# Where the halves of the weights are kept, how the block inverses are grouped, and which queue loads the weights

## The chip, the cores and the metric

The kernel runs on one core of a Trainium2 chip. A core has five engines that run side by side: TensorE (PE, matrix products into PSUM; PEld is its loading of the stationary operand), VectorE (DVE), ScalarE (ACT), GpSimd (POOL) and SyncE (SP, which issues transfers and computes nothing). Each executes its own list of instructions in order, and semaphores order the lists against one another. Transfers between DRAM and SBUF run on 16 DMA engines, whichever engine issued them.

The metric is the device time of one execution in microseconds. Of several executions the median is given.

## The reference, cut to what matters

One layer of a decoder on 2048 tokens of width 1024, all float32. A combined projection feeds three mixers; their outputs, side by side, go through w_out, a layer norm, a gated feed-forward with a depthwise convolution, and a second layer norm.

```python
proj = h @ w_in
y_a = _gated_deltanet(a_qkv, a_z, a_b, a_dec, conv_w, a_log, dt_bias, norm_w)
y_b = _dilated_window_group(b_qkv)
y_c = _diff_attention_group(c_qkv, lam_vecs, diff_norm_w, lam_init)
y = jnp.concatenate([y_a, y_b, y_c], axis=-1) @ w_out
x = _layer_norm(DEEPNORM_ALPHA * x + y, ln1_g, ln1_b)
u = _causal_depthwise_conv(x @ w_up, conv_w); gate, val = jnp.split(u, 2, axis=-1)
f = (jax.nn.silu(gate) * val) @ w_down
x = _layer_norm(DEEPNORM_ALPHA * x + f, ln2_g, ln2_b)
```

The gated delta rule (4 heads of 128) is computed by chunks. In each chunk a unit lower triangular system with the matrix I + m has to be solved, where m holds products of keys, scaled and decayed, below the diagonal; then a state of 128 x 128 for each head passes from chunk to chunk:

```python
a_mat = jnp.eye(C) + m
u = triangular_solve(a_mat, v * beta);  w = triangular_solve(a_mat, k_beta * exp(g))
def step(S, inp):
    v_new = u_i - w_i @ S
    o = q_i @ S + qk_i @ v_new
    S = S * exp(gl_i) + kt_i.T @ v_new
```

## The kernel before, in words

The 2048 tokens are four blocks of 512. Each product with a weight of 1024 x 128 (`Dense.product`, lines 182 to 184) is 8 x 3 matmuls of 512 columns: weight and activation are both split into a rounded high half and the rest, the low half, and three of the four cross products are added up.

`Dense.weights` brings a weight's halves into SBUF. On the raw path (lines 129 to 133) it loads 512 KB (`wraw`), ScalarE casts the high half (`whi`, line 132) and POOL subtracts it to get the low half (`wlo`, line 133). Where the weight has a key and `dn.keep` is set, both halves are also stored to DRAM (line 137), and a later use of the same weight loads the two halves, 512 KB each, with no arithmetic (lines 124 to 128, the kept path). `keep` is set from job A1 on (line 1292). All loads and stores are issued by SyncE. The buffers of weights are seven tiles of 512 KB (`NW`), shared by raw tiles and halves.

The work is a list of jobs in three stages (`FIRST`, `SECOND`, `THIRD`, lines 1341 to 1343):

- A0 to A3: projection of one block for the two attention mixers, eight products and the values (lines 628 to 630, which take each of the four `w_val` weights twice); 12 different weights in all.
- G0 to G3: projection of one block for the delta rule, 16 products, each followed by a convolution on VectorE (lines 336 to 344), and for queries and keys a square that POOL splits (lines 350 and 352).
- i0 to i3 (`invert`): for the four chunks of 128 tokens of a block, the products of keys (line 426), the mask with decay, and the inverses of the 32 x 32 blocks on the diagonal. These are solved on VectorE for all heads and chunks of the block at once, one block in one partition, so on 64 partitions, by 31 steps of a multiplication (line 441) and a subtraction (line 443). The blocks go through DRAM to be regrouped (`blk_d`, `x_d`).
- b0 to b7 (`merge`): for two chunks, the 32 x 32 inverses are put together into 128 x 128 inverses on TensorE.
- p0 to p7 (`prepare`), r0 to r7 (`recur`): for two chunks, transposes and query-key products, and then the recursion, whose state passes from r0 to r7 in order.
- d and w: the two attentions of a block; c0: the first pool is closed and the feed-forward's constants begin; o0: w_out and the first norm for block 0; t0: its transpose; f0 to f3: feed-forward of a block, in which the next block's w_out is done as well.

The list gives priorities and not times. A scheduler, which simulates the program as it is built, places each engine's instructions in an order of its own, so that products of a later job stand between those of an earlier one; that order is fixed when the kernel runs. `flush` emits the small pieces of work that were put off.

## Time and profile before

| | |
|---|---|
| median of 3 runs | 3292.46 us (3285.46 to 3297.71) |
| the profiled execution | 3287.69 us, span of its instructions 3285.8 us |
| PE busy | 3039.0 us, 92% |
| DVE busy | 1940.7 us, 59% |
| ACT busy | 1251.7 us, 38% |
| POOL busy | 493.0 us, 15% |
| mean granted TensorE clock | 0.955 |
| moved by DMA | 701.06 MB, 213 GB/s |

A row of a view by stretches gives the length, the busy microseconds of each engine with the number of instructions, the granted TensorE clock as a share of full speed, the mean busy share of the 16 DMA engines, and GB/s. A row of a view of groups gives line, engine, operation, output<-input tiles, shapes and count; then busy us and mean ns of one; then the engine's idle time just before them and what ended it. A row of a view of waits says which instruction waited for which: us in all, times, longest. SPq is SyncE's list.

### The profile page before, as it was taken

Reading aid. Unit: us, or ns where it says so; the run is one execution under the profiler, and the core shown is the slowest. Engines: PE = TensorE matmul, PEld = TensorE weight load, DVE = VectorE, ACT = ScalarE, POOL = GpSimd, SP = SyncE. Lnnn points to the kernel's source line nnn. Section 1 sums busy time; section 2 is a strip of 40 time slices with the busy share of each in tenths; the row PEclk is TensorE's granted clock in tenths of the full one; section 3 lists DMA queues with packets and bytes.
Section 4 is the critical chain, followed back from the end, with each engine's and each line's share of the span. In section 5 each row is a group of like instructions: output and inputs, shape, how many; then the busy total and the mean of one; then the engine's idle time right before and its main releaser. Section 6 shows DMA issues by size and latency. Waiting matters only on the chain.

```text
span 3285.8 us, 41437 instructions
## 1 busy us (share of the span) xinstructions
PE 3039.0 (92%) x14476; PEld 2335.1 (71%) x14476; DVE 1940.7 (59%) x3738; ACT 1251.7 (38%) x2735; POOL 493.0 (15%) x342
## 2 busy tenths in 40 slices
PE   7888687999978888998999999999999999999998
PEld 5666576787767667666776667777788666788887
DVE  2564177858544536755887645565897444474446
ACT  2644143353324315644655422232655333221113
POOL 3452252111102003333312000000000000000001
PEclk8899898999988989999999999999999999999999
DMA  6437776766778878766785655555775444665553
GB/s 190 144 132 263 262 257 218 222 208 200 242 253 276 289 246 265 245 225 209 269 281 198 232 187 177 180 184 173 238 261 201 148 162 144 209 236 192 192 188 139
DMA packets 365281, 701.06 MB, mean 213 GB/s; under 512 B 63024, under 2 KB 189488, under 8 KB 364304
## 3 DMA queue, kind: packets, MB, share of 16 engines
q1 hardware_dynamic: 365072, 698.41, 64.0%
q8 instruction: 115, 1.88, 0.2%
q14 instruction: 94, 0.77, 0.1%
HBM read 525.99 MB, written 172.16 MB: 212 GB/s over the span
## 4 chain that ended last, share of the span: by engine, by line
PE 57%; DMA 7%; DVE 4%; ACT 2%; issue 2%; SPq 1%; POOL 0%; ACTq 0%; POOLq 0%; DVEq 0%
PE d L184 9%; PE d L183 9%; PE d L182 9%; PE rp L1131 6%; PE rp L1132 6%; PE rp L1134 5%; PE bank L791 4%; PE bank L806 2%; DMA wraw<-in_w_up 2%; DMA wlo<-wlo_d 2%; PE bank L970 1%; PE bank L740 1%; PE bank L977 1%; PE bank L931 1%; DMA wraw<-in_w_down 1%
## 5 line engine op out<-in xcount | busy, mean ns | idle before, releaser
L182 PE MATMUL d<-xhi,whi 128*128 128x512 f32 x2144 | 872.4, 408 | 54.7 <-DVE i_halo L336 18.1
L184 PE MATMUL d<-xhi,wlo 128*128 128x512 f32 x2144 | 866.4, 404 | 22.4 <-DMA wlo<-wlo_d 18.2
L183 PE MATMUL d<-xlo,whi 128*128 128x512 f32 x2144 | 864.9, 403 | 1.8 <-DVE xlo L145 1.7
L182 PEld LDWEIGHTS d<-xhi,whi 128*128 128x128 f32 x2144 | 416.9, 195 | 164.0 <-issue 20.3
L133 POOL TENSOR_TENSOR wlo<-wraw,whi 128x1024 fp32r<-128x1024 f32 x137 | 337.1, 2461 | 1207.7 <-ACT whi L132 1067.8
L184 PEld LDWEIGHTS d<-xhi,wlo 128*128 128x128 f32 x2144 | 415.9, 194 | 131.8 <-DMA wlo<-wlo_d 20.4
L183 PEld LDWEIGHTS d<-xlo,whi 128*128 128x128 f32 x2144 | 416.6, 194 | 105.8 <-issue 18.2
L1131 PE MATMUL rp<-whi,hhi 128*128 128x512 f32 x704 | 278.6, 400 | 6.0 <-DVE r L1141 2.3
L1132 PE MATMUL rp<-wlo,hhi 128*128 128x512 f32 x704 | 279.3, 397 | 0.0
L1134 PE MATMUL rp<-whi,hlo 128*128 128x512 f32 x672 | 263.0, 397 | 0.0
L132 ACT CAST whi<-wraw 128x1024 fp32r<-128x1024 f32 x137 | 143.6, 1048 | 281.0 <-DMA wraw<-in_w_gdn 65.2
L749 ACT ACTIVATE bank<-bank,nm 128x512 f32<-128x512 f32 (+3 forms) x320 | 190.3, 595 | 110.8 <-DVE nm L745 72.7
L745 DVE TENSOR_REDUCE nm<-bank 128x1 f32<-128x512 f32 (+3 forms) x288 | 165.4, 596 | 72.6 <-PE bank L740 70.4
L1063 ACT COPY ub<-d 128x512 f32<-128x512 f32 x172 | 100.7, 586 | 265.4 <-PE d L184 264.7
L812 DVE SCALAR_TENSOR_TENSOR pd<-pe,f_nlam,pd 128x512 f32<-128x512 f32 (+3 forms) x160 | 123.5, 786 | 124.4 <-ACT pe L808 81.5
L816 POOL TENSOR_SCALAR_AFFINE_SELECT pd<-pd 128x128 f32<-128x128 f32 x64 | 29.8, 472 | 1018.0 <-DVE pd L812 990.6
L1131 PEld LDWEIGHTS rp<-whi,hhi 128*128 128x128 f32 x704 | 133.2, 189 | 43.4 <-issue 6.3
L1132 PEld LDWEIGHTS rp<-wlo,hhi 128*128 128x128 f32 x704 | 133.3, 189 | 35.0 <-issue 8.5
L1141 DVE TENSOR_TENSOR r<-r,rp 128x512 f32<-128x512 f32 x152 | 102.3, 684 | 84.1 <-PE rp L1134 77.4
L1134 PEld LDWEIGHTS rp<-whi,hlo 128*128 128x128 f32 x672 | 127.0, 189 | 33.0 <-issue 6.5
L1064 DVE COPY c_halo<-d 128x2 f32<-128x2 f32 x172 | 26.8, 156 | 205.2 <-ACT ub L1063 205.0
L1068 DVE SCALAR_TENSOR_TENSOR yg<-ub,c_taps,yg 128x512 f32<-128x512 f32 x176 | 144.8, 823 | 3.6
(280 smaller groups left out, 4723.2 us busy)
## 6 DMA issues: line engine op xcount, KB each, us to landing
whi<-whi_d SPq DMA_DIRECT2D x291, 512.0 KB
wlo<-wlo_d SPq DMA_DIRECT2D x291, 512.0 KB
whi_d<-whi SPq DMA_DIRECT2D x101, 512.0 KB
wlo_d<-wlo SPq DMA_DIRECT2D x101, 512.0 KB
ks<-fk_d SPq DMA_DIRECT2D x160, 196.0 KB
wraw<-in_w_up SPq DMA_DIRECT2D x43, 512.0 KB
wraw<-in_w_gdn SPq DMA_DIRECT2D x32, 512.0 KB
wraw<-in_w_down SPq DMA_DIRECT2D x25, 512.0 KB
```

The lines of the kernel that those rows point to most:

```text
L132: nc.scalar.copy(hi, raw)
L133: nc.gpsimd.tensor_tensor(out=lo, in0=raw, in1=hi, op=ALU.subtract)
L182: nc.tensor.matmul(out=ps, lhsT=whi[:, k], rhs=xhi[k], start=(k == 0), stop=False)
L183: nc.tensor.matmul(out=ps, lhsT=whi[:, k], rhs=xlo[k], start=False, stop=False)
L184: nc.tensor.matmul(out=ps, lhsT=wlo[:, k], rhs=xhi[k], start=False, stop=(k == KD - 1))
L745: nc.vector.tensor_reduce(out=o, in_=s[:, 0:nf], axis=mybir.AxisListType.X, op=ALU.min)
L749: nc.scalar.activation(out=s[:, 0:n], in_=s[:, 0:n], func=AF.Exp, scale=-1.0, bias=o, accum_out=den[:, b, m, qt : qt + 1])
L791: nc.tensor.matmul(out=po[64 * hh : 64 * hh + 64, q0:], lhsT=v[:, 64 * hh : 64 * hh + 64], rhs=pd[hh][:, q0:], start=start, stop=stop)
L1068: nc.vector.scalar_tensor_tensor(out=yc, in0=ub[:, j : j + TB], scalar=self.taps[:, mt, j : j + 1], in1=yc, op0=ALU.mult, op1=ALU.add)
L1131: nc.tensor.matmul(out=ps, lhsT=hi[:, sl], rhs=whi, start=first, stop=False)
L1132: nc.tensor.matmul(out=ps, lhsT=hi[:, sl], rhs=wlo, start=False, stop=last and lo is None)
L1134: nc.tensor.matmul(out=ps, lhsT=lo[:, sl], rhs=whi, start=False, stop=last)
```

## The change

- Loads of weights, raw tiles and kept halves, are issued by POOL (`nc.gpsimd.dma_start`) and no longer by SyncE. Stores of halves stay with SyncE.
- `keep` is set at job c0 and no longer at A1. In the new order c0 stands behind G3, ahead of i1. So A1, G1, G2 and G3 take the raw path without stores; A3, and after it o0 and the feed-forward, store and re-use the halves.
- `invert` takes the eight chunks of two blocks at once, on 128 partitions. There are two calls, i0 (blocks 0 and 1) and i1 (blocks 2 and 3). The scratch of a step's multiplication lies in the part of the coefficient tile that is used up, from step 5 on; for steps 0 to 4 it is a tile `ft` that it shares with the squares of `recur`.
- `merge` and the jobs' bookkeeping follow the pairs (`turn % 4`, `n // 4`), `flush` is also called ahead of a G job, and the order of `SECOND` is new.

```diff
--- before.py
+++ after.py
@@ -124,10 +124,10 @@
         if key in self.kept:
             parts = put("whi"), put("wlo")
             for part, d in zip(parts, self.kept[key]):
-                nc.sync.dma_start(out=cast(part), in_=cast(shape(d)))
+                nc.gpsimd.dma_start(out=cast(part), in_=cast(shape(d)))
             return parts
         raw = own(F32, "wraw")
-        nc.sync.dma_start(out=raw, in_=src)
+        nc.gpsimd.dma_start(out=raw, in_=src)
         hi, lo = put("whi"), put("wlo")
         nc.scalar.copy(hi, raw)
         nc.gpsimd.tensor_tensor(out=lo, in0=raw, in1=hi, op=ALU.subtract)
@@ -411,14 +411,15 @@
             nc.gpsimd.affine_select(out=m, in_=m, pattern=[[0, H], [1, P]], compare_op=ALU.is_ge,
                                     fill=0.0, base=w - 1, channel_multiplier=-1)
 
-        def invert(t):
-
-            qk_d = cols.blocks[t][0]
+        def invert(pair):
+
+
             ms = []
-            blk_d = tc.dram_tile([4, 4 * H, 32, 32], F32, name="blk_d")
-            for c in range(4):
+            blk_d = tc.dram_tile([4, 8 * H, 32, 32], F32, name="blk_d")
+            for n in range(8):
+                t, c = 2 * pair + n // 4, n % 4
                 k = p2.tile([P, H, C], F32, tag="v", name="k", bufs=NV)
-                nc.sync.dma_start(out=k, in_=qk_d[:, :, 0, c * C : (c + 1) * C])
+                nc.sync.dma_start(out=k, in_=cols.blocks[t][0][:, :, 0, c * C : (c + 1) * C])
                 m = p2.tile([P, H, P], F32, tag="m0", name="m0", bufs=NM)
                 decay(m, t, 0, c)
                 kk = bank("kk")
@@ -427,23 +428,25 @@
                 nc.vector.tensor_tensor(out=m, in0=kk, in1=m, op=ALU.mult)
                 for b in range(4):
                     bs = slice(32 * b, 32 * b + 32)
-                    nc.sync.dma_start(out=blk_d[b, c * H : (c + 1) * H].rearrange("q j i -> j q i"), in_=m[bs, :, bs])
+                    nc.sync.dma_start(out=blk_d[b, n * H : (n + 1) * H].rearrange("q j i -> j q i"), in_=m[bs, :, bs])
                 ms.append(m)
             xb = p2.tile([P, 32, 32], F32, tag="fx", name="fx", bufs=1)
-            fs = p2.tile([P, 32, 32], F32, tag="fs", name="fs", bufs=1)
-            mb, tmp = fs[0:64], fs[64:P]
+            mb = p2.tile([P, 32, 32], F32, tag="fs", name="fs", bufs=1)
             nc.sync.dma_start(out=mb, in_=blk_d.rearrange("b q j i -> (b q) j i"))
-            nc.gpsimd.memset(xb[0:64], 0.0)
-            nc.gpsimd.memset(xb[0:64].rearrange("p i c -> p (i c)")[:, 0:1024:33], 1.0)
+            nc.gpsimd.memset(xb, 0.0)
+            nc.gpsimd.memset(xb.rearrange("p i c -> p (i c)")[:, 0:1024:33], 1.0)
             for j in range(31):
                 n = 31 - j
                 rows, cls = slice(j + 1, 32), slice(0, j + 1)
-                nc.vector.tensor_tensor(out=tmp[:, rows, cls], in0=mb[:, j, rows].unsqueeze(2).broadcast_to([64, n, j + 1]),
-                                        in1=xb[0:64, j, cls].unsqueeze(1).broadcast_to([64, n, j + 1]), op=ALU.mult)
-                nc.vector.tensor_tensor(out=xb[0:64, rows, cls], in0=xb[0:64, rows, cls], in1=tmp[:, rows, cls], op=ALU.subtract)
-            nc.vector.tensor_copy(xb[64:P], xb[0:64].rearrange("p i c -> p c i"))
-            x_d = tc.dram_tile([2, 4, 4 * H, 32, 32], F32, name="x_d")
-            nc.sync.dma_start(out=x_d, in_=xb)
+                used = mb.rearrange("p j i -> p (j i)") if j > 4 else p2.tile([P, 136], F32, tag="ft", name="ft", bufs=1)
+                tmp = used[:, 0 : n * (j + 1)].rearrange("p (a b) -> p a b", a=n)
+                nc.vector.tensor_tensor(out=tmp, in0=mb[:, j, rows].unsqueeze(2).broadcast_to([P, n, j + 1]),
+                                        in1=xb[:, j, cls].unsqueeze(1).broadcast_to([P, n, j + 1]), op=ALU.mult)
+                nc.vector.tensor_tensor(out=xb[:, rows, cls], in0=xb[:, rows, cls], in1=tmp, op=ALU.subtract)
+            nc.vector.tensor_copy(mb, xb.rearrange("p i c -> p c i"))
+            x_d = tc.dram_tile([2, 4, 8 * H, 32, 32], F32, name="x_d")
+            nc.sync.dma_start(out=x_d[0], in_=xb)
+            nc.sync.dma_start(out=x_d[1], in_=mb)
             return ms, x_d
 
         def prepare(t, hb):
@@ -481,7 +484,7 @@
         def merge(turn, ms, x_d):
 
             xt = xts[turn % NXT]
-            at = 2 * (turn % 2)
+            at = 2 * (turn % 4)
             qs = slice(at * H, (at + 2) * H)
             for b in range(4):
                 bs = slice(32 * b, 32 * b + 32)
@@ -554,7 +557,7 @@
                 on = p2.tile([P, H, P], F32, tag="on", name="on")
                 nc.vector.tensor_tensor(out=on, in0=po1, in1=ea[:, 1, 2 * hb + ci].unsqueeze(2).broadcast_to([P, H, P]), op=ALU.mult)
                 nc.vector.tensor_tensor(out=on, in0=po2, in1=on, op=ALU.add)
-                junk = p2.tile([P, P], F32, tag="junk", name="junk", bufs=1)
+                junk = p2.tile([P, 136], F32, tag="ft", name="junk", bufs=1)[:, 0:P]
                 for h in range(H):
                     nc.scalar.activation(out=junk, in_=on[:, h], func=AF.Square, accum_out=sso[:, ci, h : h + 1])
                 on_all.append(on)
@@ -582,7 +585,7 @@
                 dn.flush()
                 inverse[n] = invert(n)
             elif job[0] == "b":
-                merged[n] = merge(n, *inverse[n // 2])
+                merged[n] = merge(n, *inverse[n // 4])
             elif job[0] == "p":
                 ready[n] = prepare(n // 2, n % 2)
             elif job[0] == "r":
@@ -1262,6 +1265,7 @@
             if job[0] == "A":
                 run(pr.project(n, blocks))
             elif job[0] == "G":
+                dn.flush()
                 run(gi.project(n))
             elif job[0] == "w":
                 run(dw.block(n))
@@ -1269,6 +1273,7 @@
                 run(df.block(n))
             elif job[0] == "c":
                 dn.flush()
+                dn.keep = True
                 early.close()
                 ff = Ffn(ctx, tc, I, y_d, out, dn, ap)
             elif job[0] == "o":
@@ -1289,7 +1294,6 @@
                 psy = first.enter_context(tc.tile_pool(name="psy", bufs=6 - NFIRST, space=PSUM))
                 dn.ps = Turns(psd, psd, psy) if NFIRST == 5 else Turns(psd, psy)
             for job in FIRST[1:]:
-                dn.keep = dn.keep or job == "A1"
                 emit(job)
         with ExitStack() as second:
             dn.ps = Turns(psd, psd, second.enter_context(tc.tile_pool(name="psx", bufs=1, space=PSUM)))
@@ -1339,7 +1343,7 @@
 NZ = 1
 LAG_PD = 2
 FIRST = "A0 G0 A1 G1 d0 w0".split()
-SECOND = "i0 b0 p0 b1 p1 r0 i1 p2 r1 p3 b2 r2 G2 i2 b3 b4 b5 r3 p4 G3 c0 r4 i3 p5 r5 p6 p7 b6 b7 r6 r7 A3 o0".split()
+SECOND = "i0 b0 p0 b1 p1 r0 b2 p2 r1 G2 b3 p3 r2 G3 c0 i1 r3 p4 p5 b4 b5 r4 b6 r5 A3 p6 p7 b7 r6 r7 o0".split()
 THIRD = "w1 d1 A2 t0 d2 w2 w3 d3 f0 f1 f2 f3".split()
```

## The prediction

> **What bounds the kernel now.** I read the busy time of each engine by stage first, with stage borders where the job lists change hands: 0 to 125 us is A0, 250 to 400 A1, 400 to 560 G1, 560 to 880 G2 and G3 with the first recursions, 880 to 1090 A3, o0 and the last of them, then w1 and A2, and from 1250 the feed-forward blocks. Each row gives length, busy us of PE, PEld, DVE, ACT and POOL, the granted clock, the DMA share and GB/s.
>
> ```profile
> 0.00:125.00 125.00, 91.50 (x320) 67.51 (x320) 40.09 (x128) 54.79 (x120) 42.62 (x28) 0.86 0.60 181
> 250.00:400.00 150.00, 117.35 (x567) 87.06 (x566) 45.99 (x105) 44.06 (x81) 30.61 (x16) 0.89 0.78 258
> 400.00:560.00 160.00, 128.66 (x646) 104.71 (x644) 116.56 (x190) 61.25 (x130) 65.74 (x43) 0.88 0.76 251
> 560.00:880.00 320.00, 304.23 (x2049) 255.08 (x2048) 229.47 (x491) 131.48 (x344) 54.97 (x64) 0.96 0.68 216
> 880.00:1090.00 210.00, 171.61 (x1030) 140.39 (x1029) 96.25 (x213) 65.00 (x173) 30.11 (x20) 0.88 0.80 266
> 0.00:1250.00 1250.00, 1061.50 (x5823) 846.24 (x5824) 687.51 (x1416) 456.75 (x1026) 297.50 (x221) 0.91 0.70 227
> 1250.00:3285.80 2035.80, 1977.47 (x8655) 1488.89 (x8653) 1253.17 (x2322) 794.93 (x1709) 195.49 (x121) 0.98 0.61 205
> 3100.00:3200.00 100.00, 100.00 (x441) 82.52 (x440) 46.34 (x80) 16.93 (x37) 0.00 (x0) 1.00 0.53 189
> ```
>
> TensorE bounds the feed-forward part: 58 us idle in 2036. The last row gives its pace, 100/441 = 0.227 us for a 128x512 matmul, so 24 of them, one projection product, take 5.44 us. Before 1250 us TensorE idles 1250 - 1061.5 = 188.5 us, and the clock of 0.91 costs up to 0.09 x 1250 = 112 us more. Only there is much to win. What those stalls wait for (waits of TensorE in four stretches: us in all, times, longest), first 0 to 120, then 250 to 400, 400 to 560, 880 to 1250:
>
> ```profile
> PE bank L740 <- DMA ks<-fk_d: 10.6, 3, 5.6
> PE vp L628 <- ACT whi L132: 5.8, 2, 5.6
> ...
> PE vp L628 <- ACT whi L132: 10.8, 2, 6.5
> PE d L182 <- ACT whi L132: 5.9, 1, 5.9
> PE vp L629 <- DMA wlo<-wlo_d: 4.9, 1, 4.9
> ...
> PE d L182 <- DVE i_halo L336: 12.3, 2, 6.2
> ...
> PE d L184 <- DMA wlo<-wlo_d: 7.9, 1, 7.9
> PE vp L629 <- DMA wlo<-wlo_d: 7.8, 2, 3.9
> PE rp L1131 <- ACT y L1124: 6.7, 4, 2.3
> PE bank L931 <- DMA qw<-wq_d: 9.6, 1, 9.6
> ```
>
> Weights come late in A1 and A3, VectorE in G1. Behind the late weights stands one queue: SyncE issues every transfer in order and itself waits, for buffers that a product still reads (L127, 389 us over the run) and for halves that are to be stored (L137, from 250 to 1250 us). The chain of waits has a load of 0.5 MB that needs 11 us to land:
>
> ```profile
> SPq L127 <- PE d L184: 389.0, 118, 9.8
> ...
> SPq L137 <- ACT whi L132: 66.7, 23, 10.5
> SPq L137 <- POOL wlo L133: 18.5, 13, 2.1
> ...
> 902.12 11.13 DMA wlo<-wlo_d
> ```
>
> **The change part by part.** The sum is made against the profiled run, 3287.69 us (span 3285.8, 1.9 around it); the median of the runs, 3292.46, stands 4.8 above it.
>
> ```profile
> whi<-whi_d SPq DMA_DIRECT2D x291, 512.0 KB
> whi_d<-whi SPq DMA_DIRECT2D x101, 512.0 KB
> L133 POOL TENSOR_TENSOR wlo<-wraw,whi 128x1024 fp32r<-128x1024 f32 x137 | 337.1, 2461 | 1207.7 <-ACT whi L132 1067.8 <-ACT ub L1062 53.1 <-DMA wlo_d<-wlo 33.1
> L132 ACT CAST whi<-wraw x137: 1027/1048/1091, 4.5 to 3240.6; 128x1024 fp32r<-128x1024 f32 x137
> L350 POOL CAST isqh<-isq 128x512 fp32r<-128x512 f32 x32 | 21.9, 684 | 149.4 <-ACT isq L348 107.9 <-PE nps L359 41.5
> L352 POOL TENSOR_TENSOR isql<-isq,isqh 128x512 fp32r<-128x512 f32 x32 | 46.2, 1445 | 2.0
> L441 DVE TENSOR_TENSOR fs<-fs,fx x124: 183/370/2408, 472.3 to 943.1; 64x31 f32<-64x31 f32 x8, 64x60 f32<-64x60 f32 x8, 64x87 f32<-64x87 f32 x8, 64x112 f32<-64x112 f32 x8
> L443 DVE TENSOR_TENSOR fx<-fx,fs 64x31 f32<-64x31 f32 (+15 forms) x124 | 50.4, 406 | 4.1
> L363 DVE TENSOR_TENSOR nsb<-nsb,nps 8x512 f32<-8x512 f32 x12 | 8.0, 669 | 2.7 <-PE nps L359 2.7
> L427 DVE TENSOR_TENSOR m<-kk,m 128x512 f32<-128x512 f32 x16 | 11.0, 687 | 11.2 <-POOL m L411 10.4 <-PE kk L426 0.7
> L559 ACT ACTIVATE junk<-on 128x128 f32<-128x128 f32 x64 | 19.8, 309 | 36.3 <-DVE on L556 35.5
> L130 SPq DMA_DIRECT2D wraw<-in_w_gdn x32: 328/381/593, 117.7 to 515.4; - x32
> 400.00:560.00 160.00, 38.71 (x36) 0.88 0.76 251
> 560.00:880.00 320.00, 57.49 (x72) 0.96 0.68 216
> ```
>
> *Halves kept later.* By the code, keeping starts at A3 instead of A1. A1 (12) and G1 (16) no longer store pairs and A3 stores its 12, so stores fall from 101 to 85 pairs. G2 and G3 (32) and net 16 more uses (A1 4, A3 12) turn from a kept pair (1 MB) into a raw load (0.5 MB): kept 291 to 243, raw 137 to 185. In A1 the traffic falls by 12 stored pairs (12.6 MB) and 4 kept loads halved (2.1 MB), 14.7 of the 258 GB/s x 150 us = 38.7 MB that the stage moves. SyncE's waits for halves to store, 66.7 + 18.5 us, shrink with the stores. TensorE's weight waits are 10.8 + 5.9 + 4.9 = 21.6 us; some of that was the first use of a weight, which stays raw, so I take three quarters: -16 (0 to -22). A3 takes A1's old form, with stores, and its weight waits today are nearly as large, 7.9 + 7.8: 0 (-16 to +6, the difference of the two).
>
> *The price in G2 and G3.* 48 more casts (48 x 1.048 = 50 us of ScalarE) and 48 more subtractions (48 x 2.46 = 118 us of POOL). The casts lie under the products (each 1.05 of 5.44 us; without that cover 50 us), the subtractions too, but the subtraction and VectorE's two-input operations hold each other up: the inverse's L441 is 370 ns at the median and 2408 at most, as long as a subtraction. The last two rows are VectorE on L341, two inputs as well: 38.71/36 = 1.08 us beside the raw loads of G1, 57.49/72 = 0.80 beside the kept pairs of G2 and G3; 0.28 x 72 gives 20 us of VectorE. G1, which loads raw, is the nearest row for G2 and G3: TensorE at 128.66/160 = 80% busy against 95%. At worst 304.23 us of work at 80% take 378, +58; at best 0. G1's share is low also through an inverse amid it, so I take +12.
>
> *Paired inverses.* Two chains of 62 VectorE operations on 128 partitions in place of four on 64. L363 on 8 partitions takes 0.669 us and L427 on 128 takes 0.687, so I give the chain's operations the same length as now: (124 x 0.423 + 50.4)/2 = 51 us of VectorE less (0 if they grew twofold). The transfers carry the same bytes in fewer, larger pieces. The chain's first five steps now share a tile with the recursion's squares (L559): at most 8 x 0.31 = 2.5 us for each of two inverses, under the products. In G1 TensorE waits 12.3 us on VectorE, in 560 to 880 it idles 320 - 304 = 16 us at all; I take 12 of these 28: -12 (0 to -28; a loss at the end of this stage is a rival below).
>
> *Loads on POOL's queue.* 185 raw loads and 2 x 243 halves, 671 issues, leave SyncE; the stores stay. The loads no longer stand behind SyncE's waits, nor the other transfers behind theirs. In A0: -8 of 10.6 + 5.8 (0 to -16). From 880 to 1250: 7.9 + 7.8 of weights, 9.6 + 6.7 of others; I take half, -15 (0 to -32). No DMA issued by POOL stands in the trace. From below it costs SyncE's issue, 0.38 us; from above POOL's own pass over such a tile, 2.46. An issue doesn't read the tile, so it is nearer to the first: 1.0. POOL's load for a product is then 2.0 us for a kept pair, 3.5 for a raw one, and 4.5 in the G jobs with half of (0.68 + 1.45) for the squares; all stay under 5.44, so nothing of it is on the path. What is queued behind a load that waits for its buffer on POOL: the next subtraction, the causal selects, the squares. They need POOL once per product at most; a buffer comes free once per product, too. In the feed-forward part, with 58 us idle, I take 0 (-15 to +15).
>
> ```profile
> L1066 DVE TENSOR_SCALAR yv<-ub,c_taps x84: 465/477/2548, 1259.4 to 3240.8; 128x512 f32<-128x512 f32 x84
> ```
>
> This row shows VectorE's one-input multiply at 477 ns, and up to 2548 when a subtraction on POOL runs: the two lock each other out. The Trainium skill (SBUF — State Buffer, section "SBUF: two separate sides") says that this lock also starves transfers issued from POOL, whose descriptors POOL writes: one of about 0.62 us took 3.1 beside VectorE copies. By that figure, an estimate, a kept pair would cost POOL 6.2 us, over the product's 5.44, and 243 of them would put some 185 us on the sum; no run here shows it.
>
> *Clock.* 39 us less idle time before 1250 us; lost clock there is 112/188 = 0.6 us for each idle one, of which I take a quarter, since the stalls are shortened and not removed: -10 (0 to -23).
>
> Sum: -16 + 0 + 12 - 12 - 8 - 15 + 0 - 10 = -49, so 3239 for a run like the profiled one, and 3243 as a median.
>
> **Rivals.**
>
> *G2 and G3 run like G1.* The 58 us of the worst case in place of 12: -49 + 46 = -3, 3290. For it: VectorE is 229/320 = 72% busy there, and every collision is paid on its chain. Against it: in 560 to 880 no inverse but i1's remains to be shared with.
>
> *The queue brings nothing.* If loads are late because the 16 engines are full (DMA share 0.78) and not because of the order of issue, -8, -15 and half the clock fall away: 3271. The Trainium skill (DMA: Bandwidth & Descriptors, "Issuing engines are not separate DMA queues") says just this, that another issuing engine saves issue time only; the waits of SyncE on buffers quoted above are no issue time, so the rows bear it out in part.
>
> *The chain after G3 sets the end (slower).* Today i2 and i3 run apart, and at 880 only r5 to r7 are left. After the change i1 needs all of G3's keys, and r4 to r7 follow it one behind the other. The rows (the first matmuls of two chunks of a recursion; one chain of an inverse, first to last):
>
> ```profile
> 923.99 1.05 PE L530 MATMUL pk<-S,qk 128*128 128x128 f32 x8
> 944.41 1.06 PE L530 MATMUL pk<-S,qk 128*128 128x128 f32 x8
> ...
> L443 DVE TENSOR_TENSOR fx<-fx,fs x31: 189/354/1124, 896.6 to 943.3; 64x31 f32<-64x31 f32 x2, 64x60 f32<-64x60 f32 x2, 64x87 f32<-64x87 f32 x2, 64x112 f32<-64x112 f32 x2
> ```
>
> A chunk takes 20.4 us, the inverse 943.3 - 896.6 = 47: 47 + 8 x 20.4 = 210 us from G3's keys to r7. It decides when TensorE has less than that left to do. Today's 880 to 1090 holds 172 us of its work; two recursions more, with their p and b, add to it (their matmuls are not grouped by job, so I bound them by 0 and by the 38 us that fill the stretch). Uncovered are 0 to 38 us, and the two recursions that move behind G3, 4 x 20.4 = 82 us, are the most that the stage can grow: 82 - 49 = +33, 3325. Against it: A3's and o0's products are free to be put into the gaps, and a chunk on a VectorE without G's convolutions should be shorter.
>
> *POOL becomes the bound (slower).* It decides when an issue on POOL costs over 5.44/2 = 2.72 us in the feed-forward part, or 5.44 - 2.46 - 1.07 = 1.9 in the G jobs. At my upper row, 2.46, only the G jobs pay, 64 x 0.56 = 36 us: 3279. At 2.9: 243 x (5.8 - 5.44) = 87 and 64 x 1.0 = 64, with half the gains left, -24: +127, 3420. Against it: 2.9 is above my upper row.
>
> **How the numbers follow.** Forecast 0.42 (alone 3215 to 3270); G2 and G3 like G1 0.21; queue without effect 0.13; chain after G3 0.13; POOL 0.11. 0.5% of 3292 is 16 us, about what a measurement of this kernel can tell. Faster means under 3276: 0.40 + 0.05 + 0.10 + 0.01 + 0.01 = 0.57. Within 3276 to 3309: 0.02 + 0.11 + 0.03 + 0.02 + 0.02 = 0.20. Slower: 0.05 of the second, 0.10 of the chain, 0.08 of POOL: 0.23. The range 3190 to 3335 leaves out POOL at 2.9 and more, and the best ends of all bounds at once.
>
> **What would show it.** A1: TensorE's waits for weights down from 21.6 us to under 10, its stage at a lower DMA share. G2 and G3: L341 on VectorE near the 38.71/36 = 1.08 us that it has in 400 to 560. The line of L443: x62 at about 0.41 us. POOL: issues near 1 us each, POOL under 60% busy in every stretch from 1250 on. If POOL is over 90% busy there, or if TensorE waits on L133 by tens of us, the forecast is wrong; also if TensorE idles over 100 us between the end of G3 and w1, since then the chain i1, r4 to r7 sets the end.

## The result, and the profile after the change

The changed kernel takes 3443.03 us (median of 4 runs, 3442.66 to 3446.48), the kernel before beside it 3288.96 us (4 runs): the ratio is 1.0483, with a 95% interval of 1.0454 to 1.0511. It is 154 us slower. The prediction had 3243 us and a range of 3190 to 3335, so it was wrong in sign, and the range did not hold the result. In the changed kernel lines from 420 on have numbers higher by 1 to 5 than before; in kernels below that load early, lines from 113 on are higher by 1 to 28 more.

From the page of the changed kernel: busy time by engine, the two DMA queues, and the loads that POOL issues, with their size and the median from issue to landing.

```profile
PE 3086.0 (90%) x14476; PEld 2346.7 (68%) x14476; DVE 1900.5 (55%) x3612; ACT 1296.3 (38%) x2781; POOL 974.3 (28%) x1057
...
q0 software_dynamic: 96624, 351.84, 30.0%
q1 hardware_dynamic: 256256, 304.62, 27.6%
...
whi<-whi_d POOLq DMA_DIRECT2D x243, 512.0 KB, 4.9
wlo<-wlo_d POOLq DMA_DIRECT2D x243, 512.0 KB, 4.0
...
wraw<-in_w_gdn POOLq DMA_DIRECT2D x64, 512.0 KB, 3.9
```

The change does what it says: 243 kept pairs, loads on a queue of their own. POOL is busy for only 28%. TensorE's work is the same 14476 matmuls, 47 us longer than before (3039.0). The rest of the longer span, 112 us, is idle time. The view by stretches tells where; first the changed kernel, in the columns of the prediction:

```profile
0.00:1400.00 1400.00, 1110.83 (x5877) 868.32 (x5877) 672.93 (x1300) 506.04 (x1081) 509.02 (x444) 0.88 0.55 175
1400.00:3444.70 2044.70, 1975.17 (x8601) 1478.36 (x8599) 1227.60 (x2313) 790.25 (x1701) 465.32 (x613) 0.98 0.60 203
...
1400.00:2000.00 600.00, 551.65 (x2065) 371.36 (x2064) 370.17 (x691) 325.30 (x715) 200.28 (x166) 0.96 0.65 214
```

and the kernel before over the same two stretches:

```profile
0.00:1400.00 1400.00, 1200.23 (x6386) 953.02 (x6387) 799.10 (x1646) 547.45 (x1241) 346.08 (x242) 0.91 0.70 230
1400.00:3285.80 1885.80, 1838.74 (x8091) 1382.11 (x8090) 1141.59 (x2092) 704.23 (x1495) 146.91 (x101) 0.99 0.60 201
```

Up to 1400 us TensorE idles 1400 - 1110.8 = 289 us in place of 200, at a clock of 0.88 in place of 0.91, and has done 509 matmuls fewer. The DMA engines are less busy on average (0.55 against 0.70), so over this stretch bandwidth is not what became short. TensorE's waits over the whole run of the changed kernel (us in all, times, longest) name what it lacks:

```profile
PE d L182 <- ACT whi L132: 47.2, 26, 7.1
PE d L184 <- POOL wlo L133: 38.9, 33, 1.8
...
PE vp L631 <- ACT whi L132: 19.6, 10, 4.7
PE vp L632 <- POOL wlo L133: 16.4, 12, 2.0
```

The same four rows of the kernel before:

```profile
PE vp L628 <- ACT whi L132: 16.6, 4, 6.5
...
PE d L182 <- ACT whi L132: 13.0, 4, 5.9
...
PE d L184 <- POOL wlo L133: 4.0, 4, 1.8
...
PE vp L629 <- POOL wlo L133: 3.3, 4, 1.2
```

These are 122 us of waits for the cast and the subtraction of a raw weight, in place of 37. "TensorE waits on L133 by tens of us" was one of the signs that the prediction named for its own failure; 38.9 + 16.4 us is that. What stands behind it is seen in POOL's own instructions in order of time (start, us, instruction; in brackets POOL's idle time before it and what ended it), at the start of job G1:

```profile
505.32 2.36 POOL L133 TENSOR_TENSOR wlo<-wraw,whi 128x1024 fp32r<-128x1024 f32 x1 [3.16 <-ACT whi L132]
507.62 0.57 POOL L130 DMA_DIRECT2D wraw<-in_w_gdn  x1
512.79 2.39 POOL L133 TENSOR_TENSOR wlo<-wraw,whi 128x1024 fp32r<-128x1024 f32 x1 [4.61 <-ACT whi L132]
515.13 0.57 POOL L130 DMA_DIRECT2D wraw<-in_w_gdn  x1
520.06 2.38 POOL L133 TENSOR_TENSOR wlo<-wraw,whi 128x1024 fp32r<-128x1024 f32 x1 [4.36 <-ACT whi L132]
522.40 0.57 POOL L130 DMA_DIRECT2D wraw<-in_w_gdn  x1
```

Read it as a loop. A load is issued; POOL comes to its next instruction, the subtraction of that same weight, and stands still until the load has landed and ScalarE has cast it; only behind the subtraction stands the next load. From one subtraction to the next are 512.79 - 505.32 = 7.5 and 520.06 - 512.79 = 7.3 us, and the parts add up to that: 3.9 us from issue to landing, 1.05 us of cast, 2.4 us of subtraction. A product needs 5.44 us, so each raw weight comes about 2 us late, while POOL is idle for more than half of the time. Before, SyncE issued the raw loads; a subtraction on POOL could hold one up where the store of its low half stood ahead on SyncE's list (8.5 us of SyncE's waits from 400 to 541 us).

### The profile page after: what moved, and what is told of

It is laid out like the page before. It is cut to its first block, busy times and chain, and to the rows that moved or that the text cites. A ratio compares the mean times of both kernels' runs of the same rounds, so it can differ in the third digit from the quotient of the medians.

```text
span 3444.7 us, 41305 instructions
## 1 busy us (share of the span) xinstructions
PE 3086.0 (90%) x14476; PEld 2346.7 (68%) x14476; DVE 1900.5 (55%) x3612; ACT 1296.3 (38%) x2781; POOL 974.3 (28%) x1057
## 5 line engine op out<-in xcount | busy, mean ns | idle before, releaser
L184 PE MATMUL d<-xhi,wlo 128*128 128x512 f32 x2144 | 870.5, 406 | 42.2 <-POOL wlo L133 38.9
L133 POOL TENSOR_TENSOR wlo<-wraw,whi 128x1024 fp32r<-128x1024 f32 x185 | 450.5, 2435 | 947.0 <-ACT whi L132 836.4
L127 POOL DMA_DIRECT2D wlo<-wlo_d x243 | 130.6, 537 | 1212.4 <-PE d L184 614.7
L132 ACT CAST whi<-wraw 128x1024 fp32r<-128x1024 f32 x185 | 193.4, 1046 | 350.1 <-DMA wraw<-in_w_gdn 88.7
L1134 PE MATMUL rp<-whi,hhi 128*128 128x512 f32 x704 | 271.0, 400 | 9.5 <-ACT whi L132 6.4
L341 DVE SCALAR_TENSOR_TENSOR yc<-ub,i_taps,yc 128x512 f32<-128x512 f32 x144 | 159.0, 1104 | 3.0
L743 PE MATMUL bank<-ks,qs 96*128 96x512 f32 (+3 forms) x320 | 113.0, 403 | 42.2 <-DMA ks<-fk_d 23.5
L127 POOL DMA_DIRECT2D whi<-whi_d x243 | 143.1, 589 | 23.1 <-PE d L184 7.7
```

The costliest lines, as they stand in the source:

```text
L127: nc.gpsimd.dma_start(out=cast(part), in_=cast(shape(d)))
L132: nc.scalar.copy(hi, raw)
L133: nc.gpsimd.tensor_tensor(out=lo, in0=raw, in1=hi, op=ALU.subtract)
L184: nc.tensor.matmul(out=ps, lhsT=wlo[:, k], rhs=xhi[k], start=False, stop=(k == KD - 1))
L341: nc.vector.scalar_tensor_tensor(out=yc, in0=ub[:, j : j + TB], scalar=self.taps[:, mt, j : j + 1], in1=yc, op0=ALU.mult, op1=ALU.add)
L1134: nc.tensor.matmul(out=ps, lhsT=hi[:, sl], rhs=whi, start=first, stop=False)
```

## The experiments

Theory L says that this loop is the loss. Its first rivals were C (the chain of the paired inverse and the last recursions behind G3, the prediction's slower rival), S (transfers issued by POOL are slow in themselves) and G (the casts and subtractions that late keeping adds in G2 and G3). One thing is to be kept in mind with all runs: the order of each engine's list is planned when the kernel is built, from what each instruction is thought to take, so an edit of a load also shifts other instructions. The medians below stand beside 3286 to 3290 us for the kernel before, measured with them; each ratio is against those runs.

### Raw loads back on SyncE

```diff
         raw = own(F32, "wraw")
-        nc.gpsimd.dma_start(out=raw, in_=src)
+        nc.sync.dma_start(out=raw, in_=src)
```

> The changed kernel with one edit: the raw loads are issued by SyncE again, the loads of kept halves stay on POOL. Theory L (the loop): with raw loads on POOL its list runs load, landing, cast, subtraction, next load, one after the other, some 8 us for each raw weight against the 5.44 us of a product; 96 raw weights stand before the end of G3, so 96 x up to 2.5 us. It expects 3250 to 3310 us, TensorE's waits on the cast of the high half and on the subtraction (86 us in the changed kernel at the first and third matmul of a product) down to under 35 us, and raw loads issued on SyncE while the subtraction before them is still to come. Rival S (transfers issued by POOL are slow in themselves): the 243 kept pairs still come from POOL, so over 3380. Rival C (the paired inverse and r4 to r7 after G3 set the end): nothing of it is changed, so over 3400, with the 61 us of idle time of TensorE in the 220 us after G3 still there.

Measured: 3320.72 us, ratio 1.0094 (1.0075 to 1.0113). One line takes 122 of the 154 us away. Expected were 3250 to 3310, so it is 11 us above L's range, and 60 to 80 below what S and C expected. TensorE's waits at the first and third matmul of a product fall from 86 to 26 us (18.1 + 8.0), as L had it.

### All loads back on SyncE

```diff
-                nc.gpsimd.dma_start(out=cast(part), in_=cast(shape(d)))
+                nc.sync.dma_start(out=cast(part), in_=cast(shape(d)))
...
-        nc.gpsimd.dma_start(out=raw, in_=src)
+        nc.sync.dma_start(out=raw, in_=src)
```

> The changed kernel with all loads of weights issued by SyncE again; the later keeping, the paired inverses and the new order stay. Theory L: within 25 us of the kernel with only the raw loads moved back, so 3240 to 3320. Rival C (order and pairs cost the time): over 3400. My forecast on record, without its terms for the queue and half of the clock, puts this kernel at 3271.

Measured: 3314.31 us, ratio 1.0073 (1.0052 to 1.0094). The queue as a whole costs 129 us, nearly all of it through raw loads. The rest of the change costs 26 us; the prediction had 3271 for it.

### The queue alone

The kernel before with the two lines of `weights` as in the change:

```diff
-                nc.sync.dma_start(out=cast(part), in_=cast(shape(d)))
+                nc.gpsimd.dma_start(out=cast(part), in_=cast(shape(d)))
...
-        nc.sync.dma_start(out=raw, in_=src)
+        nc.gpsimd.dma_start(out=raw, in_=src)
```

> The kernel before with one edit: all loads of weights are issued by POOL; keeping starts at A1, inverses are single, the old order stays. Theory L: 60 of the 96 raw weights before the end of G3 are still raw in this kernel (A0, G0, A1, G1), so 60/96 of the change's loss against all loads on SyncE, some 100 us: 3350 to 3420. Rival C: 3290 or less, since order and pairs are those of before. Rival K (late keeping alone costs it, by 48 more casts and subtractions): 3290 or less.

Measured: 3408.35 us, ratio 1.0359 (1.0339 to 1.0380). With the old order, single inverses and early keeping the queue still costs 120 us. So C and late keeping are not what makes most of the loss. By the count of raw weights before the end of G3 it should have been some 100; the feed-forward's first block, whose weights are raw in both kernels, was left out of that count.

### Early loads in the G jobs

The load of the next raw weight goes ahead of the subtraction of the present one; all loads stay on POOL.

```diff
+        def fetch(w):
+            raw = own(F32, "wraw")
+            nc.gpsimd.dma_start(out=raw, in_=w)
+            return raw
-        raw = own(F32, "wraw")
-        nc.gpsimd.dma_start(out=raw, in_=src)
+        raw = self.ahead.pop(key) if key in self.ahead else fetch(src)
+        if then and then[0] not in self.kept:
+            self.ahead[then[0]] = fetch(then[1])
         hi, lo = put("whi"), put("wlo")
...
```

> The changed kernel, all loads still on POOL, but in the four G jobs the load of the next raw weight is issued ahead of the subtraction of the present one (64 weights); the A jobs stay as they are. Theory L: the loop holds two weights, so a weight takes (0.57 + 4 + 1.05 + 2.4)/2 = 4 us, under the 5.44 of a product; two thirds of the 96 raw weights are mended, so the time falls by 60 to 130 us, to 3310 to 3385, and POOL's wait ahead of the subtraction falls from 4.4 to under 2 us in G1. Rival S (POOL's queue is slow, or POOL has too much to do): within 25 us of 3443. Rival C: within 25 us of 3443.

Measured: 3419.35 us, ratio 1.0400 (1.0378 to 1.0423): 24 us gained, 36 short of the least that L expected, and within the 25 us that S and C had allowed. The time alone would speak against L. The stages speak for it: the convolutions on VectorE follow the products of a G job, and their first and last start measure it. G0 in the changed kernel:

```profile
L341 DVE SCALAR_TENSOR_TENSOR yc<-ub,i_taps,yc x36: 725/752/2836, 183.7 to 313.0; 128x512 f32<-128x512 f32 x36
```

and with early loads in the G jobs:

```profile
L350 DVE SCALAR_TENSOR_TENSOR yc<-ub,i_taps,yc x36: 726/752/4154, 185.6 to 289.2; 128x512 f32<-128x512 f32 x36
```

129.3 us became 103.6 us; it is 106.6 us before the change. The job that was mended is as fast as it was, those that weren't are not: G0 still starts at 186 in place of 146 us, because A0 in front of it has the loop. The last convolution of G3 starts 55 us earlier than in the changed kernel (867.4 against 922.4), but from 1400 to 2000 us, where the first feed-forward block brings its raw weights, TensorE does the same 2065 matmuls as in the changed kernel (2297 with all loads on SyncE), and more than half of the gain is lost again by the end. So the test had to be made with all raw loads.

### Early loads everywhere

The same for nearly every raw weight: `then` names the next weight in the projections for attention, in the values, in w_out, w_up and w_down; for the values, say:

```diff
-                whi, wlo = dn.weights(self.I["w_val"][j], k=2, m=TB, key=("val", j))
+                then = (("val", (j + 1) % 4), self.I["w_val"][(j + 1) % 4], 2, TB) if g + j < 4 else None
+                whi, wlo = dn.weights(self.I["w_val"][j], k=2, m=TB, key=("val", j), then=then)
...
```

> The changed kernel, all loads still on POOL, but every raw load whose follower is known (A, G, w_out, w_up and w_down, nearly all 185) is issued one weight early, ahead of the subtraction of the weight before it. With the G jobs alone mended the kernel stood at 3419 us: G0 took 104 us where the changed kernel takes 130 and the kernel with raw loads on SyncE 107, but A0 (150 us before its values are done against 111) and the feed-forward's first block, with 68 raw weights, ran as slowly as in the changed kernel. Theory L (the loop load, landing, cast, subtraction on POOL is the whole loss of the queue): within 25 us of the kernel with raw loads on SyncE, 3300 to 3345. Rival S (something else of POOL's queue costs: slower landings, issue time, more collisions): over 3380, hardly better than with the G jobs alone.

Measured: 3284.68 us, ratio 0.9986 (0.9970 to 1.0001). The whole 154 us is gone with every load still on POOL, and with it 36 us that the kernel with raw loads on SyncE still had; that is 15 us below L's range, so early loads do more than mend the loop. Its page has the same work on POOL and nearly the same landing times as the changed kernel (974.3 us busy, 3.9 us to landing there):

```profile
PE 3009.3 (92%) x14476; PEld 2321.8 (71%) x14476; DVE 1956.9 (60%) x3612; ACT 1303.1 (40%) x2781; POOL 973.7 (30%) x1057
...
wraw<-in_w_gdn POOLq DMA_DIRECT2D x64, 512.0 KB, 4.1
```

So S does not make the 154 us: same instructions, same transfers, nearly the same times of each; only the order on POOL's list differs. Whether POOL's queue costs something smaller is asked further below. POOL's list in this kernel, again in G1:

```profile
402.69 2.41 POOL L139 TENSOR_TENSOR wlo<-wraw,whi 128x1024 fp32r<-128x1024 f32 x1 [2.39 <-ACT whi L138]
405.04 0.57 POOL L132 DMA_DIRECT2D wraw<-in_w_gdn  x1
405.63 1.29 POOL L361 TENSOR_TENSOR isql<-isq,isqh 128x512 fp32r<-128x512 f32 x1
406.88 2.39 POOL L139 TENSOR_TENSOR wlo<-wraw,whi 128x1024 fp32r<-128x1024 f32 x1
409.22 0.57 POOL L132 DMA_DIRECT2D wraw<-in_w_gdn  x1
411.36 2.77 POOL L139 TENSOR_TENSOR wlo<-wraw,whi 128x1024 fp32r<-128x1024 f32 x1 [1.57 <-ACT whi L138]
```

The second and third subtraction follow the one before after 4.2 and 4.5 us, under a product's 5.44: the weight was on its way before POOL took up the one ahead of it. TensorE's waits for raw weights in products and values (whole run) are these and one of 2.2 us, 28 us in place of the 122 above:

```profile
PE d L190 <- POOL wlo L139: 9.7, 4, 4.5
...
PE vp L648 <- POOL wlo L139: 8.3, 2, 6.5
...
PE d L188 <- ACT whi L138: 7.5, 1, 7.5
```

### Late keeping alone, and paired inverses alone

First the kernel before with `keep` set at c0:

```diff
             elif job[0] == "c":
                 dn.flush()
+                dn.keep = True
...
-                dn.keep = dn.keep or job == "A1"
```

> The kernel before with one edit: keep is set at c0 and no longer at A1; the order, the inverses and SyncE's queue are those of before. The changed kernel with all loads on SyncE is 26 us slower than the kernel before; it has this edit and the paired inverses with the new order. Theory C (the chain i1, r4 to r7 behind G3 makes those 26 us, and the later keeping gains by itself, as G1's end came 44 us earlier there): 3255 to 3280. Rival G (the extra casts and subtractions in G2 and G3 make them): 3300 to 3330. My forecast on record for this part, -16 +12 and a quarter microsecond or so of clock for each idle one, is 3280 to 3286.

Measured: 3308.78 us, ratio 1.0071 (1.0043 to 1.0100): slower, as G had it. Then the inverses and the new order, with keeping from A1 and SyncE's loads, here as an edit of the changed kernel with all loads on SyncE:

```diff
                 dn.flush()
-                dn.keep = True
...
             for job in FIRST[1:]:
+                dn.keep = dn.keep or job == "A1"
```

> The kernel before with the paired inverses and the new order of jobs alone: keep is set at A1, all loads are SyncE's. Theory C: slower, 3300 to 3345, with more of TensorE's idle time behind G3's end than the 40 us of before (244 us with 204 us busy). Rival G (the extra casts and subtractions make the 26 us): 3265 to 3285, by the 51 us of VectorE's time that the pairs save. My forecast on record for this part, -12, is 3277.

Measured: 3276.56 us, ratio 0.9966 (0.9949 to 0.9982): a little faster, close to the 3277 of the forecast. So it is the later keeping, and not the chain behind G3, that loses when all loads are SyncE's. The two alone add up to 18 - 14 = +4 us, together they cost 26; the 22 us between were not traced.

VectorE's side of the paired inverses, by groups in the changed kernel (from step 5 on, and steps 0 to 4 with the tile `ft`):

```profile
L445 DVE TENSOR_TENSOR fx<-fx,fs 128x156 f32<-128x156 f32 (+15 forms) x52 | 29.1, 559 | 1.3
L443 DVE TENSOR_TENSOR fs<-fs,fx 128x156 f32<-128x156 f32 (+15 forms) x52 | 22.3, 429 | 1.0
L443 DVE TENSOR_TENSOR ft<-fs,fx 128x31 f32<-128x31 f32 (+4 forms) x10 | 3.5, 354 | 5.1 <-DMA fs<-blk_d 4.9
L445 DVE TENSOR_TENSOR fx<-fx,ft 128x31 f32<-128x31 f32 (+4 forms) x10 | 2.9, 292 | 0.2
```

29.1 + 22.3 + 3.5 + 2.9 = 57.8 us, against 124 x 0.423 + 50.4 = 102.9 before: 45 us less, where the prediction had 51.

### Kept loads alone on POOL

The kernel before with the kept path's line as in the change, raw loads on SyncE:

```diff
-                nc.sync.dma_start(out=cast(part), in_=cast(shape(d)))
+                nc.gpsimd.dma_start(out=cast(part), in_=cast(shape(d)))
```

> The kernel before with one edit: the loads of kept halves are issued by POOL, raw loads stay on SyncE. A kept load has no landing behind it on POOL's list, so theory L has no loss here: 3265 to 3300. Rival S (POOL's queue is slow in itself): over 3330. My forecast on record gave the queue -15 in the stage from 880 to 1250 us, mostly through kept loads: 3274.

Measured: 3309.20 us, ratio 1.0072 (1.0047 to 1.0097). That is slower than L expected by 9 us and far from S. The forecast had 3274. A kept load has no loop of the kind above, and still the queue gains nothing with it but costs 19 us. Nearly all of that arises between the end of G1 and the end of G3:

```profile
541.00:871.00 330.00, 298.66 (x2005) 245.99 (x2003) 230.70 (x475) 126.05 (x320) 91.11 (x127) 0.93 0.65 204
```

The kernel before takes 312 us there, with 2008 matmuls (its row stands under "Halves kept later" below). In this stretch POOL stands still for 84 us, in 22 waits, until a product gives free the buffer that a kept load needs, and the squares of G2 and G3 stand behind such loads on its list; the loads in turn stand behind casts that wait 44 us for ScalarE's squares. The prediction had put what is queued behind a load that waits for its buffer at nothing. Which of these waits makes the 18 us was not settled.

### Early loads on SyncE

Early loads had done more than mend the loop, so the next question was what they are worth without POOL's queue. All loads on SyncE, late keeping, paired inverses, new order; against the kernel with early loads everywhere:

```diff
-                nc.gpsimd.dma_start(out=cast(part), in_=cast(shape(d)))
+                nc.sync.dma_start(out=cast(part), in_=cast(shape(d)))
...
-            nc.gpsimd.dma_start(out=raw, in_=w)
+            nc.sync.dma_start(out=raw, in_=w)
```

> The kernel in which every raw load is issued one weight early, with all loads of weights on SyncE in place of POOL (late keeping, paired inverses, new order). It tells what the 30 us between all loads on SyncE as they were (3314 us) and early loads on POOL (3285 us) come from. Theory E (the early issue alone): 3275 to 3295. Theory Q (POOL's queue, whose loads don't stand behind SyncE's stores and other transfers, as my forecast on record had it with -23 and some clock): 3300 to 3320.

Measured: 3250.83 us, ratio 0.9889 (0.9860 to 0.9918), better than what either theory expected: 63 us under the same kernel without early loads, and 34 us under early loads on POOL. Theory Q, and with it the prediction's term for the queue, falls: SyncE's queue is the faster one once loads are issued in time. Of the 129 us that POOL's queue costs in the changed kernel, 34 are left when raw loads are early; the other 95 go with the order on the list.

Then keeping from A1, by the same edit as for the paired inverses alone, with early loads and all loads on POOL:

> Early raw loads, all loads on POOL, paired inverses and the new order, but keep is set at A1 as in the kernel before. If the parts add up: late keeping alone cost 18 us, so 3285 - 18 = 3267; if the queue's gain grows with the number of kept loads, to 3245. Rival (kept loads on POOL cost something where keeping is early, as in the kernel before with kept loads alone on POOL, 19 us slower): 3280 to 3300.

Measured: 3255.12 us, ratio 0.9903 (0.9883 to 0.9923), 12 us below the sum of the parts and clear of the rival; and on SyncE:

> The same with all loads on SyncE: early raw loads, paired inverses, new order, keep at A1. The paired inverses without early loads stood at 3277 us. Theory E: 3245 to 3260, as early loads take 30 us more off. Theory Q: 3270 to 3285, no better than without early loads.

Measured: 3246.01 us, ratio 0.9866 (0.9843 to 0.9889), as E had it. And the kernel before with early loads and nothing else, the core of the edit in `weights`:

```diff
-        raw = own(F32, "wraw")
-        nc.sync.dma_start(out=raw, in_=src)
+        raw = self.ahead.pop(key) if key in self.ahead else fetch(src, k, m)
+        if then and then[0] not in self.kept:
+            self.ahead[then[0]] = fetch(*then[1:])
...
```

> The kernel before with one edit: every raw load whose follower is known is issued one weight early. All loads are SyncE's, keep is set at A1, inverses are single, the order is the old one. If early loads gain by themselves, 137 raw weights have them here against 185 in the kernel with late keeping, where they took 63 us (3314 to 3251): 63 x 137/185 = 47, so 3240 to 3265 us. Rival (their gain needs the paired inverses and the new order, which stand at 3277 without them and at 3246 with them, 31 us): 3257 to 3290.

Measured: 3246.25 us, ratio 0.9868 (0.9833 to 0.9903), within the 3240 to 3265 expected. One edit, without pairs, order, late keeping or POOL's queue, is as good as any mixture. The paired inverses' gain does not add to it.

Part of what early loads mend in the kernel before is seen on SyncE's list. Near the start of G1 of the kernel before, with the lines between left out:

```profile
398.63 0.32 SPq L137 DMA_DIRECT2D whi_d<-whi  x1
399.04 0.38 SPq L130 DMA_DIRECT2D wraw<-in_w_gdn  x1
...
406.19 0.32 SPq L137 DMA_DIRECT2D whi_d<-whi  x1
406.60 0.38 SPq L130 DMA_DIRECT2D wraw<-in_w_gdn  x1
```

and near the start of the same job with early loads:

```profile
399.77 0.33 SPq L132 DMA_DIRECT2D wraw<-in_w_gdn  x1
...
405.21 0.33 SPq L132 DMA_DIRECT2D wraw<-in_w_gdn  x1
...
410.66 0.33 SPq L132 DMA_DIRECT2D wraw<-in_w_gdn  x1
```

Before, a raw load stands right behind the store of the high half of the weight before it, and that store has to wait for the cast: a loop of load, landing, cast and store. The cast starts at 405.12 us, 6.1 us after the load, and takes 1.04; from load to load it is 7.6 us. With early loads the loads follow here at 5.44 and 5.45 us, the pace of a product. So the kernel before has a loop of the same kind as the changed kernel, on another engine's list.

That loop is only a part, though. Over the whole of G1 its 16 loads follow at 8.4 us on average before and still at 7.2 with early loads. SyncE waits on its list for more than casts: from 400 to 541 us it is 27 us for casts, 21 for results of VectorE that are to be stored, 9 for subtractions, and around 451 to 466 us the issues of other transfers, the inverse's above all, fill it. From G1's first convolution to its last it is 122.4 us before and 117.0 with early loads, 5 of the 39 us gained. A0 gains as well, where nothing is stored: 11 us at its first values, 9 at its last. TensorE's waits for weights hardly fall, from 75 to 70 us: those for raw weights from 41 to 27, while those for kept halves rise from 34 to 43. The run shows that the place of the raw loads is what gains; through which waits was not traced to the end.

### What POOL's queue costs when loads are early

Raw loads early on SyncE, kept loads on POOL, late keeping; against the kernel with early loads everywhere:

```diff
-            nc.gpsimd.dma_start(out=raw, in_=w)
+            nc.sync.dma_start(out=raw, in_=w)
```

> Early raw loads on SyncE, kept loads on POOL (late keeping, paired inverses, new order). It splits the 34 us between all loads on POOL (3285) and all on SyncE (3251), both with early raw loads. Theory H (kept loads that wait for a buffer on POOL hold up the subtractions and other work behind them): 3275 to 3290. Rival W (the raw loads are what POOL's list still holds up, for instance in A0, where the values are done at 111 us against 102): 3250 to 3262.

Measured: 3262.17 us, ratio 0.9919 (0.9889 to 0.9950). Of the 34 us between POOL's queue and SyncE's, 23 come with the raw loads and 11 with the kept ones; the 11 lie within the intervals of the two. That is W's upper edge; whether H has a part is not clear from it. In A0 the first values are done at 97.6 us with SyncE's raw loads and at 111.6 us with POOL's, the last at 122.6 and 130.1, so some of the 23 us arise there; what delays them in A0 was not traced further.

## Why the prediction was wrong, step by step

| part of the sum | forecast | measured alone, against the kernel before |
|---|---|---|
| halves kept later, with the price in G2 and G3 | -16 + 0 + 12 = -4 | +18 (ratio 1.0071) |
| paired inverses and new order | -12 | -14 (ratio 0.9966) |
| loads on POOL's queue | -8 - 15 + 0 = -23 | +120 (ratio 1.0359) |
| TensorE's clock | -10 | lower: 0.943 over the run in place of 0.955 |

**The step that failed** is "POOL's load for a product is then 2.0 us for a kept pair, 3.5 for a raw one, and 4.5 in the G jobs ...; all stay under 5.44, so nothing of it is on the path". The numbers in it are not the fault. The issue was put at 1.0 us and takes 0.53 to 0.57, the subtraction takes its 2.4, and POOL stays at 28%. But busy time is not what an in-order list is bound by when one of its own instructions waits for what another has started. The load and the subtraction of one weight came to stand on one list, with the landing and the cast between them, and 0.57 + 2.4 us of work became a loop of 7.4. The next sentence of the prediction asked the right question the wrong way round: "What is queued behind a load that waits for its buffer on POOL". It should also have asked what the load is queued behind.

**The bound of POOL's issue** was taken between 0.38 and 2.46 us, and these rows of the changed kernel (shortest, median and longest in ns, first and last start) lie near the lower end:

```profile
L130 POOL DMA_DIRECT2D wraw<-in_w_gdn x64: 570/570/599, 163.7 to 899.6; - x64
...
L127 POOL DMA_DIRECT2D wlo<-wlo_d x243: 530/531/938, 1083.5 to 3410.8; - x122
```

The Trainium skill (SBUF — State Buffer, section "SBUF: two separate sides") warns that VectorE's copies starve transfers issued by POOL. Its 3.1 us are the time of a whole transfer; the prediction weighed them as POOL's own time for an issue. The issues here show nothing of it: of the 486 loads of kept halves the longest issue took 0.94 us, with VectorE busy for 55% of the run. Their landings took 4.6 us at the median and 12.4 at most; the prediction's row of one that SyncE issued has 11.1.

**Gain of the queue.** The prediction took the waits on SyncE's list as the reason for late weights, and a second queue as the cure. The first half holds in so far as another place on the same list gains 39 us; the second does not hold: with early loads POOL's queue is 34 us slower than SyncE's with late keeping and 9 us with keeping from A1. The Trainium skill (DMA: Bandwidth & Descriptors, section "Issuing engines are not separate DMA queues") says that another issuing engine saves the time of issue only. The runs go with it: no pair of kernels that differs in the queue alone is faster on POOL (3321 against 3314, 3309 against 3290, 3285 against 3251, 3255 against 3246; in the first and the last of these the intervals of the two overlap).

**Halves kept later.** G1's last convolution starts at 515 us with late keeping alone, 25 us earlier than before (540.1), so the gain in A1 and G1 was there, and larger than the 16 us forecast. It was paid back in G2 and G3. That kernel takes 359 us from the end of G1 to the end of G3,

```profile
516.00:875.00 359.00, 312.38 (x2055) 258.32 (x2056) 281.26 (x486) 158.23 (x361) 131.75 (x91) 0.91 0.47 142
```

where the kernel before has 312:

```profile
541.00:853.00 312.00, 289.13 (x2008) 241.08 (x2007) 224.47 (x475) 126.28 (x323) 52.75 (x62) 0.95 0.68 215
```

That is +47. The forecast had +12, so this term was mis-sized, and the rival "G2 and G3 run like G1", with +58, had it nearly right. Part of the price is that raw loads come late. With paired inverses, the new order and all loads on SyncE the same stretch reads as follows: keeping from A1, late keeping, and then the same two with early loads.

```profile
523.00:798.00 275.00, 265.98 (x1730) 221.61 (x1729) 181.93 (x386) 117.74 (x296) 51.40 (x51) 0.98 0.71 231
497.00:821.00 324.00, 281.40 (x1752) 231.22 (x1750) 228.88 (x386) 143.94 (x325) 134.16 (x87) 0.93 0.47 144
498.00:776.00 278.00, 267.39 (x1734) 223.27 (x1733) 183.87 (x386) 116.69 (x295) 47.92 (x51) 0.98 0.68 223
479.00:783.00 304.00, 269.43 (x1721) 224.11 (x1721) 227.72 (x385) 144.10 (x324) 126.42 (x82) 0.96 0.48 147
```

(They hold some 300 matmuls fewer than the two rows above, since the second inverse's jobs have moved behind G3 here.) Late keeping costs 324 - 275 = 49 us there without early loads and 304 - 278 = 26 with them, so about half of the price went with the early loads. The other half stays, and the reason that the prediction and the rival gave, VectorE's convolution of two inputs beside subtractions, may be in it: with early loads that line takes 80.00 us for 73 of them under late keeping (1.10 us each) and 59.42 us for 73 under early keeping (0.81), 21 us more. That these 21 us make the 26 was not shown. Over the whole run late keeping costs 3314 - 3277 = 38 us without early loads and only 3251 - 3246 = 5 with them, as G1 then ends 19 us earlier (479 in place of 498) and G2 and G3 pay 26.

**Paired inverses.** Right in size and sign when alone, and VectorE's chain is shorter by nearly what the prediction worked out (45 us against 51). That run also has the new order of jobs, so how much of its 14 us the inverses make was not separated.

**The other rivals.** The chain behind G3 does not set the end: paired inverses alone are faster than before. "POOL becomes the bound" had a time near the result, 3420, for a reason that did not occur: it needed an issue of 2.9 us. "The queue brings nothing" was nearer to the truth about the queue than the forecast, but none of the rivals held the loop.

## What to carry to other kernels

When a transfer is moved to another engine's queue, write down that engine's list for two rounds and find what the transfer now stands behind. If the engine's own work on the data stands between one load and the next, the loop is landing time plus all work on the way, whatever the engine's busy share says; issue the next load ahead of the work on the present one. Look for such loops first on the queue in use: here moving the raw loads up on SyncE's list gained 1.3%, and no other queue was needed.

## What the runs showed that was not expected

- A load of 512 KB costs POOL 0.53 to 0.57 us of its list and lands 3.9 to 5.2 us after its issue (medians of the groups); no issue of a kept half took longer than 0.94 us beside a VectorE at 55%.
- POOL's queue lost to SyncE's in each of four comparisons that leave the order of loads alone, by 6 to 34 us (the two smallest with intervals that overlap), though SyncE also carries all other transfers. Why it loses with loads issued early is open; 23 of the 34 us come with the raw loads and 11 with the kept ones.
- The gain does not grow evenly with the loads that are mended: 64 of 185 raw loads gave 24 us, nearly all of them 158.
